# Layer 0 attention with two heads' scores in the two row halves of the array, and the side work at fixed places

## The chip, the cores and the metric

The kernel is one program on one core of a Trainium2 chip. It runs a diffusion backbone of two layers over 2048 latent tokens and 256 context tokens. The metric is the device time of one execution in microseconds (us). The engines have short names here: PE is the TensorE (its matmuls), PEld its weight loads, DVE the VectorE, ACT the ScalarE, POOL the GpSimd, and SP the engine that issues most DMAs. Matmul results are written to PSUM, which the kernel divides into 8 banks of 128 partitions by 512 fp32 values.

## The reference, cut to what matters

Layer 0 runs two mixers side by side on the same normalised input and adds their outputs through one output projection. Mixer A is attention with 8 heads; a query or key has 96 numbers, 64 without and 32 with a rotary part. Mixer B is linear attention in both directions with decay gates, in chunks.

```python
def mla_heads(q_lat, kv_lat, k_rope, q_norm, w_uq, kv_norm, w_ukv, q_gain, k_gain, rope):
    q = jnp.dot(rms_norm(q_lat, q_norm), w_uq).reshape(bsz, n, A_HEADS, A_QK)        # 8 heads x 96
    kv = jnp.dot(rms_norm(kv_lat, kv_norm), w_ukv).reshape(bsz, n, A_HEADS, A_NOPE + A_V)
    ...
    q = jnp.concatenate([q[..., :A_NOPE], apply_axial_rope(q[..., A_NOPE:], cos, sin)], axis=-1)
def block_attention(q, k, v, scale):
        s = jnp.einsum('bqhd,bkhd->bhqk', qi, k, preferred_element_type=jnp.float32) * scale
        p = jax.nn.softmax(s, axis=-1).astype(v.dtype)
        return jnp.einsum('bhqk,bkhd->bqhd', p, v)
def even_mixer(...):
    a_x = block_attention(q_x, [k_x, k_c], [v_x, v_c], scale)      # latent queries, all keys
    b_x, b_c = gla_bidirectional(gla_inputs(...), gla_inputs(...)) # mixer B
    y = jnp.dot(jnp.concatenate([a * silu(za), rms_norm(b) * silu(zb)], axis=-1), w_out)
    a_c = block_attention(q_c, k_c, v_c, scale)                    # context queries, context keys
# mixer B, one chunk: cumulative decay b, then
        att = jnp.where(mask, jnp.einsum('bhld,bhmd->bhlm', q_t, k_t), 0.0)
        o = jnp.einsum('bhld,bhde->bhle', q_t, state) + jnp.einsum('bhlm,bhme->bhle', att, vi)
        state = state * jnp.exp(b_last)[..., 0, :, None] + jnp.einsum('bhld,bhle->bhde', k_dec, vi)
```

## The kernel before, in words

**Precision.** A matrix product is made of reduced-precision fp32 parts: an operand is split into a high part and a low part, and a product is the sum of three matmuls, high by high, high by low and low by high.

**Stages.** `even_latent` makes queries and keys and writes them to the scratch tensors `QT` and `KT` in DRAM. `even_rest` makes the other projections and, woven into them, the row maxima of the scores (`maxes`); the negated maxima become row 96 of `QT`, and row 96 of `KT` holds ones, so that the first score matmul subtracts the maximum by itself. `even_mix` holds the stage that the change rewrites: attention (mixer A), mixer B (`gla`) and the splitting of the 16 units of `w_out` into high and low parts. Then `project` multiplies by `w_out`, and layer 1 follows.

**Attention, `even_attention`.** Heads go in 4 pairs `j`. Each pair has 5 query blocks `nb`: one of 256 context queries with 2 key tiles, and four of 512 queries with 18 key tiles of 128 keys each. That is 4 x (2 + 4 x 18) = 296 steps, and in each step both heads of the pair do one key tile. For one head a step has three matmuls into one PSUM bank `st` (L972 with 97 rows, L973 and L974 with 96 rows), one exponential on ACT into a tile `apt`, and on DVE one addition into the running sum `acc` (L963). `st` has 3 banks. When six steps are pending, four of them are multiplied with the values (L914, two heads in the two column halves of the array, plain fp32) into a bank `av`. `finish` (L842 to L857) takes the denominators with a matmul of the sums (L846, bank `den`), then Ln and Exp on ACT, three operations on DVE, one on POOL, and the store into `RT`. Two further banks, `gl`, belong to mixer B. Together these are 3 + 2 + 1 + 2 = 8 banks.

**Mixer B, `gla`.** 18 chunks of 128 tokens. `front` and `back` make a chunk's low-rank input (L714), gate logits (L720), log gates, cumulative decays (L731, L735), transposes (L758), masked scores within the chunk (L768, row halves of 64, plain fp32), values (L777) and state (L783). Then two scans run over the chunks, forward on POOL and backward on DVE (L806 to L808), and a second pass adds the carried state (L822), normalises, gates, and writes `RT`.

**Order.** `even_attention` is a generator: the code starts it, then emits all of `gla`, then the 16 weight splits, and then runs the rest of attention. A scheduler decides, from its own costs, where each instruction of these streams stands on its engine's queue. Every engine works its queue in order. `issue_after(x)` puts an instruction behind `x` on its engine. SP's queue is in order too, and in the built program each DMA on it waits until the eighth before it has landed.

Of the kernel before, what the change touches and what calls it, by code (L numbers as in the profile page):

```python
# [10 lines left out]
F32 = mybir.dt.float32  # L11
# [6 lines left out]
P = 128  # L18
# [70 lines left out]
class Kern:  # L89
# [311 lines left out]
    def even_latent(self, ws, wrest, kept):  # L401
        nc, tc = self.nc, self.tc
        self.QT = self.scr("QT", (A_HEADS, 2, A_QK + 1, T), F32)
        self.KT = self.scr("KT", (A_HEADS, 2, A_QK + 1, T), F32)
        self.Vn = self.scr("Vn", (P, NT, 512), F32)
        self.Un = self.scr("Un", (NT, P, 1568), F32)
        with ExitStack() as es:
# [34 lines left out]
            one = self.tl(sp, [P, Q_LORA], "sql", bufs=1)  # L442
            nc.gpsimd.memset(one[:8], 1.0)
            for o in range(0, T, Q_LORA):
                nc.sync.dma_start(self.KT[:, 0, A_QK, o : o + Q_LORA], one[:8])
# [104 lines left out]
            def fin(t):  # L550
                qn, kn = nat.pop(t)
                for z, (src, dst) in enumerate(((qn, self.QT), (kn, self.KT))):
                    col = 2 * z + (0 if t < NCT else 1)
                    for h2 in range(2):
                        ps = self.tl(pp, [P, 4, P], "tp")
                        for j in range(4):
# [6 lines left out]
                        nc.sync.dma_start(  # L563
                            dst[h2 * 4 : h2 * 4 + 4, :, :A_QK, t * P : t * P + P].rearrange("h s d t -> d (h s) t"),
                            hl[:A_QK].rearrange("d h s t -> d (h s) t").bitcast(F32))
# [42 lines left out]
    def even_rest(self, ws, win, hT):  # L608
        nc = self.nc
        self.zaT = self.scr("zaT", (4, P, T), F32)  # L610
        with ExitStack() as es:
# [33 lines left out]
            def maxes():  # L645
                for h in range(A_HEADS):
                    k = self.tl(sp, [P, T], "mk", F32R, bufs=2)
                    nc.sync.dma_start(k[:A_QK].bitcast(F32), self.KT[h, 0, :A_QK])
                    m = self.tl(sp, [P, NT, 5], "mm")
                    nc.vector.memset(m[:], -3e38)  # L650
                    for t in range(NT):
                        if t % 6 == 0:
                            q = self.tl(sp, [P, 768], "mq", F32R)
                            nc.sync.dma_start(q[:A_QK].bitcast(F32), self.QT[h, 0, :A_QK, t * P : t * P + 768])
# [13 lines left out]
                    nc.gpsimd.dma_start(self.QT[h, 0, A_QK].rearrange("(t p) -> t p", p=P), r[:NT].bitcast(F32))  # L668
# [9 lines left out]
    def gla(self, gp, gs, g1, gd, pp, tag):  # L678
# [25 lines left out]
        z4 = lambda a: a.rearrange("p (h z d) -> p h z d", z=2, h=H)  # L704

        def front(c):

            u = self.tl(g1, [P, 1056], "gu")
            nc.sync.dma_start(u[:], self.Un[c, :, :1056])
            gq, gk, gv = u[:, :256], u[:, 256:512], u[:, 512:1024]  # L710
            ps = bank()
            u3 = self.tl(gs, [P, 3, 32], "gu3")
            g.tensor_copy(u3[:], u[:, 1024:1056].unsqueeze(1).to_broadcast([P, 3, 32]))
            nc.tensor.transpose(ps[:96, :P], u3[:].rearrange("p n d -> p (n d)"), self.ident[:])  # L714
            r = rT[c % 2]
            self.act(r[:96, :], ps[:96, :P])
            nc.vector.tensor_tensor(out=r[32:64, :], in0=ps[32:64, :P], in1=r[32:64, :], op=ALU.subtract)
            yield
            lg = bank()
            nc.tensor.matmul(lg[:], r[:], gw[:], start=True, stop=True)  # L720
            e = self.tl(gs, [P, 512], "ge")
            self.act(e[:], lg[:], AF.Abs)
            self.act(e[:], e[:], AF.Exp, scale=-1.0)
# [65 lines left out]
        for _ in front(0):  # L789
            pass  # L790
# [946 lines left out]
```

## Time and profile before

The runs took 3657.13 us (median of 3, 3656.99 to 3663.05). The profiled execution spans 3650.5 us from its first to its last instruction.

| what | us |
|---|---|
| median of the runs | 3657.13 |
| span of the profiled execution | 3650.5 |
| latent stage (0 to 660 us) | 660 |
| rest and row maxima (660 to 1093.6) | 433.6 |
| attention with mixer B and the weight splits (1093.6 to 1974.1) | 880.5 |
| projection and layer 1 (1974.1 to the end) | 1676.4 |
| PE busy over the span | 3552.0 (97%) |

A row of a timeline gives the start and the length of an instruction, or of several that were merged (x8). Matmuls are pipelined, and the length of one reaches past the start of the next; what a matmul costs is therefore the distance between starts. "97*128" means 97 rows and 128 columns of the array, "97x512" the tile that moves through. In a row of a group stand its busy time, the mean of one in ns, the idle time of the engine just before it, and what ended that. A matmul in plain fp32 appears as two records.

### The profile page before, as it was taken

Reading aid. Unit: us, or ns where it says so; the run is one execution under the profiler, and the core shown is the slowest. Engines: PE = TensorE matmul, PEld = TensorE weight load, DVE = VectorE, ACT = ScalarE, POOL = GpSimd, SP = SyncE. Lnnn points to the kernel's source line nnn. Section 1 sums busy time; section 2 is a strip of 40 time slices with the busy share of each in tenths; the row PEclk is TensorE's granted clock in tenths of the full one; section 3 lists DMA queues with packets and bytes.
Section 4 is the critical chain, followed back from the end, with each engine's and each line's share of the span. In section 5 each row is a group of like instructions: output and inputs, shape, how many; then the busy total and the mean of one; then the engine's idle time right before and its main releaser. Section 6 shows DMA issues by size and latency. Waiting matters only on the chain. (4 is left out here: it accounts for less than half of the span.)

```text
span 3650.5 us, 51811 instructions
## 1 busy us (share of the span) xinstructions
PE 3552.0 (97%) x18404; PEld 2747.6 (75%) x18404; DVE 2355.2 (65%) x4846; ACT 1433.2 (39%) x2740; POOL 1234.9 (34%) x1376
## 2 busy tenths in 40 slices
PE   8999999999999999999999999999899999999899
PEld 6988987888886666665656887888788887555577
DVE  4677666888876766678765435455488784666732
ACT  5445551111115555555654214444422222555510
POOL 1433330101011211221311224333344442888763
PEclk9999999999999999999999999999999999999999
DMA  7455463222243232342632544545734446898672
GB/s 259 142 156 155 135 177 110 87 75 84 69 116 86 66 107 66 89 125 66 179 110 93 184 139 141 159 146 155 245 126 144 131 133 181 212 223 220 190 235 97
DMA packets 365780, 512.25 MB, mean 140 GB/s; under 512 B 26081, under 2 KB 245297, under 8 KB 359618
## 3 DMA queue, kind: packets, MB, share of 16 engines
q1 hardware_dynamic: 320754, 417.69, 39.3%
q0 software_dynamic: 22112, 63.26, 5.7%
q10 hardware_dynamic: 22656, 27.99, 2.2%
q8 instruction: 146, 2.39, 0.3%
q14 instruction: 112, 0.92, 0.1%
HBM read 329.45 MB, written 179.37 MB: 139 GB/s over the span
## 5 line engine op out<-in xcount | busy, mean ns | idle before, releaser
L963 DVE TENSOR_TENSOR acc<-acc,apt 128x512 f32<-128x512 f32 x512 | 375.6, 756 | 168.5 <-ACT apt L106 165.6
L106 ACT ACTIVATE apt<-st 128x512 f32<-128x512 f32 (+1 forms) x592 | 343.6, 594 | 290.7 <-PE st L974 262.0
L660 DVE TENSOR_REDUCE mm<-mx 128x1 f32<-128x512 f32 (+1 forms) x656 | 388.7, 629 | 87.3 <-PE mx L659 80.0
L914 PE MATMUL av<-apt,av 128*64 128x512 f32 (+1 forms) x1184 | 280.6, 594 | 0.0
L972 PE MATMUL st<-aq,akh 97*128 97x512 f32 (+1 forms) x592 | 256.6, 434 | 8.8 <-DMA aq<-QT 4.4
L659 PE MATMUL mx<-mk,mq 96*128 96x512 f32 (+1 forms) x656 | 235.8, 373 | 5.0 <-DMA mq<-QT 3.4
L1430 POOL TENSOR_TENSOR oacc<-oacc,opt 128x576 f32<-128x576 f32 (+5 forms) x192 | 223.0, 1184 | 39.7 <-ACT rl L106 19.3
L973 PE MATMUL st<-aq,akh 96*128 96x512 f32 (+1 forms) x592 | 235.5, 398 | 0.0
L1548 DVE TENSOR_TENSOR opt<-st,tab 128x64 f32<-128x64 f32 (+10 forms) x576 | 144.6, 317 | 140.3 <-PE st L1391 63.8
L974 PE MATMUL st<-aq,akl 96*128 96x512 f32 (+1 forms) x592 | 234.4, 396 | 0.0
L106 ACT ACTIVATE u<-gm 128x352 f32<-128x352 f32 (+1 forms) x140 | 68.6, 498 | 373.2 <-PE gm L131 210.6
L1307 DVE CUSTOM_DVE_ANT_1 mx<-mx,mtab 128x217 f32<-128x217 f32 (+12 forms) x576 | 184.2, 338 | 40.1 <-PE mx L1301 30.9
L914 PEld LDWEIGHTS av<-apt,av 128*64 128x64 f32 x1184 | 80.5, 137 | 153.6 <-issue 152.3
L972 PEld LDWEIGHTS st<-aq,akh 97*128 97x128 f32 x592 | 113.0, 191 | 99.1 <-issue 50.5
L106 ACT ACTIVATE opt<-opt 128x930 f32<-128x930 f32 (+7 forms) x129 | 104.2, 810 | 110.7 <-DVE opt L1548 102.6
L659 PEld LDWEIGHTS mx<-mk,mq 96*128 96x128 f32 x656 | 121.2, 188 | 16.8 <-DMA mk<-KT 3.8
L974 PEld LDWEIGHTS st<-aq,akl 96*128 96x128 f32 x592 | 113.9, 193 | 25.6
L973 PEld LDWEIGHTS st<-aq,akh 96*128 96x128 f32 x592 | 114.4, 193 | 17.1
L129 PE MATMUL gm<-w1h,hhi 128*128 128x512 f32 x288 | 116.3, 404 | 6.8 <-ACT onat L106 6.8
L106 ACT ACTIVATE x<-px,modB,modA 128x128 f32<-128x128 f32 x272 | 99.3, 468 | 56.9 <-PE px L339 54.4
L129 PE MATMUL gm<-w0h,hhi 128*128 128x512 f32 x288 | 116.3, 404 | 2.0 <-DVE hhi L351 1.9
L807 POOL TENSOR_TENSOR gsf<-gsf,D 64x512 f32<-64x512 f32 x17 | 25.1, 1477 | 271.4 <-DVE D L784 271.4
(492 smaller groups left out, 9962.1 us busy)
## 6 DMA issues: line engine op xcount, KB each, us to landing
q<-Q SPq DMA_DIRECT2D x48, 512.0 KB
H<-x ACTq DMA_DIRECT2D x36, 512.0 KB
adaw<-ada_w SPq DMA_DIRECT2D x64, 256.0 KB
x<-H SPq DMA_DIRECT2D x32, 512.0 KB
wraw<-w_od SPq DMA_DIRECT2D x64, 256.0 KB
K1t<-okt POOLq DMA_DIRECT2D x32, 512.0 KB, 7.6
kt<-K1t SPq DMA_DIRECT2D x32, 512.0 KB
mtab<-rpb_q SPq DMA_DIRECT2D x16, 899.0 KB
```

Source lines behind the costliest of these rows:

```text
L106: return self.nc.scalar.activation(out, in_, func, **kw)
L129: self.nc.tensor.matmul(out, lh(k), rh(k), start=j == 0, stop=False)
L659: mm = nc.tensor.matmul(ps[:, :w], q[:A_QK, (t % 6) * P : (t % 6) * P + P], k[:A_QK, k0 : k0 + w], start=True, stop=True)
L660: nc.vector.tensor_reduce(out=m[:, t, n : n + 1], in_=ps[:, :w], axis=AX.X, op=ALU.max)
L914: nc.tensor.matmul(O[j, nb][i * 64 : i * 64 + 64, :w], V[j, kt // TT][:, kt % TT, i * 64 : i * 64 + 64], pts[i][:, :w], start=n == 0, stop ...
L963: nc.vector.tensor_tensor(out=acc[i][:, :w], in0=a[:, :w], in1=pts[i][:, :w], op=ALU.add)
L972: nc.tensor.matmul(ps[:, :w], kh[: A_QK + 1, i, kq], qh[: A_QK + 1, :w], start=True, stop=False)
L973: nc.tensor.matmul(ps[:, :w], kh[:A_QK, i, kq], ql[:A_QK, :w], start=False, stop=False)
L974: mm = nc.tensor.matmul(ps[:, :w], kl[:A_QK, i, kq], qh[:A_QK, :w], start=False, stop=True)
L1307: nc.vector.tensor_tensor_reduce(out=s, in0=s, in1=tb[:, ri : ri + rn, ci : ci + cn], scale=1.0, scalar=-3e38, op0=ALU.add, op1=ALU.max, a ...
L1430: self.psum = nc.gpsimd.tensor_tensor(out=a, in0=a, in1=pts[:, :, a0 - r0 : a1 - r0, :], op=ALU.add)
L1548: bias = nc.vector.tensor_tensor(out=pt[:, d[0], d[1]], in0=ps[:, d[0], d[1]], in1=tabs[j][i][:, ri : ri + rn, ci : ci + cn], op=ALU.add)
```

## The change

**Scores.** Queries and keys are written to other scratch tensors: `QA`/`KA` (64 numbers without the rotary part), `QC`/`KC` (the 32 rotary numbers) and `QM` (the negated maxima). A pair's key tiles now hold head 0 in rows 0 to 63 and head 1 in rows 64 to 127. A step's score for one head is five matmuls with 64 rows (the last with 33): high by high, high by low and low by high of the 64 numbers; then the high rotary key, loaded twice, against the high and the low rotary query; then the low rotary key with the row of ones against the high rotary query with the row of maxima. The two heads' matmuls alternate between the two row halves and write two banks of one `st` tile. There are two such tiles (four banks). One ACT instruction makes both heads' exponentials (1024 columns), and one DVE instruction adds both heads' sums. For the context block nothing is added on DVE: its denominators are summed by PE.

**Places.** `gla` and the weight splits become a generator `side` that names the kind of place which its next piece wants. The cycle is four steps long: two steps, the place "middle", two steps, and `flush`, which has a place before the value matmuls ("before", "turn", "unit", "second") and one behind them ("after"). At a place the next piece is emitted if it wants that kind. A due denominator (`end`) stands in a flush too, and then a "second" piece waits. The denominators and the context block's output share the two banks `gl` with mixer B. Of a chunk, the place "before" takes `decays`, "turn" the transposes, "middle" the scores within the chunk, "after" the values, the forward scan, the low-rank input and the logits. The second pass takes one "second" place for each chunk. Each of the first 15 weight units takes one "unit" place; the sixteenth is split by `project`'s caller. What is left when attention ends is emitted behind it.

**Moved between engines.** Of mixer B, the copies of the low-rank input and of the values' output and the first step of the log gates go from ACT to DVE; the subtraction of the log gates, the addition of the two masked scores and the last operation of the backward scan go from DVE to POOL; the sum of squares goes from DVE to ACT (four instructions with an accumulator).

In the diff below, the first part makes the scratch tensors; the second, in `fin`, makes three stores of one; then come mixer B's pieces, the loads of a pair's keys (five for one; the low parts take three for one and the queries seven for two), `place` and `flush`, one step, and the weight units in `even_mix`. What was one load in the row maxima is two there.

```diff
-        self.QT = self.scr("QT", (A_HEADS, 2, A_QK + 1, T), F32)
-        self.KT = self.scr("KT", (A_HEADS, 2, A_QK + 1, T), F32)
+        self.QA, self.KA = [self.scr(n, (2, A_HEADS, A_NOPE, T), F32) for n in ("QA", "KA")]
+        self.QC, self.KC = [self.scr(n, (A_HEADS, 2, A_ROPE, T), F32) for n in ("QC", "KC")]
+        self.QM = self.scr("QM", (A_HEADS, T), F32)
...
-                        nc.sync.dma_start(
-                            dst[h2 * 4 : h2 * 4 + 4, :, :A_QK, t * P : t * P + P].rearrange("h s d t -> d (h s) t"),
-                            hl[:A_QK].rearrange("d h s t -> d (h s) t").bitcast(F32))
+                        for part in range(2):
+                            nc.sync.dma_start(da[part, hs, :, ts].rearrange("h d t -> d h t"), hl[:A_NOPE, :, part, :].bitcast(F32))
+                        nc.sync.dma_start(dc[hs, :, :, ts].rearrange("h s d t -> d (h s) t"),
+                                          hl[A_NOPE:A_QK].rearrange("d h s t -> d (h s) t").bitcast(F32))
...
+        for c in range(NT + 1):
+            if c:
+                yield "middle"
+                within(c - 1)
+            if c < NT:
+                yield "before"
+                decays(c)
+                softplus(c + 1)
+            if c:
+                yield "after"
+                values(c - 1)
+                scan(c - 1, slice(0, 64), g, g, "gsf")
+                inputs(c + 1)
+            if c < NT:
+                yield "turn"
+                turn(c)
+                yield "after"
+                low_rank(c + 3)
+                logits(c + 2)
+                fetch(c + 4)
...
+        for n in range(NT + 1):
+            yield "second"
+            if n:
+                write(order[n - 1])
+            if n < NT:
+                carried(order[n])
+                if n + 1 < NT:
+                    reads(order[n + 1])
+                squares(order[n])
+                if n + 1 < NT:
+                    back(order[n + 1])
+                gated(order[n])
...
+                dma(kh[:, 0, a:b], self.KA[0, 2 * j : 2 * j + 2, :, ts].rearrange("h d t -> (h d) t"))
+                for i in range(2):
+                    for o in (i * 64, i * 64 + 32):
+                        dma(kh[o : o + 32, 1, a:b], self.KC[2 * j + i, 0, :, ts])
...
+        def place(kinds, mm, *marks):
+            nonlocal want
+            if want not in kinds:
+                return mm
+            self.woven = mm
+            with ExitStack() as es:
+                for x in (mm, *marks):
+                    es.enter_context(self.tc.issue_after(x.ins))
+                want = next(side, None)
+            return self.woven
+
+        def flush(mm, *marks):
+            was, due = want, [x for x in late if x[0] or want != "before"]
...
+            mm = place(("before", "turn", "unit") if due else ("before", "turn", "unit", "second"), mm, *marks)
...
+                        mm = end(*x[1:])
...
+                        mm = tail(*p)
...
+            return place(("after",), mm, *marks)
...
-                    for i in range(2):
-                        qh, ql = Q[:, 2 * i, :], Q[:, 2 * i + 1, :]
-                        ps = self.tl(pp, [P, 512], "st", bufs=3)
-                        nc.tensor.matmul(ps[:, :w], kh[: A_QK + 1, i, kq], qh[: A_QK + 1, :w], start=True, stop=False)
-                        nc.tensor.matmul(ps[:, :w], kh[:A_QK, i, kq], ql[:A_QK, :w], start=False, stop=False)
-                        mm = nc.tensor.matmul(ps[:, :w], kl[:A_QK, i, kq], qh[:A_QK, :w], start=False, stop=True)
-                        pt = self.tl(ap, [P, 512], "apt", bufs=14)
-                        self.act(pt[:, :w], ps[:, :w], AF.Exp, scale=A_SCALE)
-                        pts.append(pt)
-                    add(n, pts)
+                    ps = self.tl(pp, [P, 2, 512], "st", bufs=2)
+                    terms = ((kh, 0, 0, 64), (kh, 0, 1, 64), (kl, 0, 0, 64), (kh, 1, 2, 64), (kl, 1, 3, 33))
+                    with self.tc.issue_after(mm.ins) if mm else ExitStack():
+                        for m, (k, kb, qb, r) in enumerate(terms):
+                            for o in (0, 64):
+                                mm = nc.tensor.matmul(ps[:, o // 64, :w], k[o : o + r, kb, kq], Q[o : o + r, qb, :w], start=m == 0, stop=m == 4)
+                    pts = self.tl(ap, [P, 2, 512], "apt", bufs=7)
+                    marks = [self.act(pts[:, :, :w], ps[:, :, :w], AF.Exp, scale=A_SCALE)]
...
+                    if len(pend) == 4:
+                        mm = place(("middle",), mm, *marks)
+                    elif len(pend) == 6:
+                        mm = flush(mm, *marks)
...
+                    for u in range(2 * KD):
+                        if waiting:
+                            self.split_unit(w, *waiting.pop())
+                        if u < 2 * KD - 1:
...
+                            waiting.append((u, self.load_unit(u, self.tl(g1, [P, 512], "gG", bufs=2)), place))
+                            yield "unit"
...
+            u = 2 * KD - 1
+            self.split_unit(w, u, self.load_unit(u, self.tl(sp, [P, 512], "py")), [self.tl(g1, [P, 512], "gG", F32R, bufs=2)[:] for _ in range(2)])
```

More of the change, by code (lines that the diff above doesn't have):

```diff
@@ L727, in front @@
             G4 = G[:].rearrange("p (h z d) -> p h z d", z=2, h=H)
-            yield
             mid = bank()
@@ L989, in even_attention @@
[L989 to L994 removed]
+                    if len(pend) == 4:
+                        mm = place(("middle",), mm, *marks)
+                    elif len(pend) == 6:
+                        mm = flush(mm, *marks)
+                    if nb == 4 and j < 3:
+                        if n == 2:
+                            for b in range(2):
+                                early[b], _ = queries(j + 1, b)
+                        if n % TT == TT - 1 and n < NT - 1:
+                            load(keys(j + 1, n // TT + 1), low(j + 1, n // TT))
@@ L996, in ln_exp @@
+        while pend or late:
+            mm = flush(mm, *marks)
+        for _ in side:
+            pass
     def ln_exp(self, after, es):
```

365 lines of the change are left out of this document (218 added, 147 removed).

## The prediction

> **What bounds the kernel now.** I read the page's totals first, then busy time by stage, then PE's timeline, the other engines' groups in the stage, and the places where PE is idle.
>
> ```profile
> span 3650.5 us, 51811 instructions
> PE 3552.0 (97%) x18404; PEld 2747.6 (75%) x18404; DVE 2355.2 (65%) x4846; ACT 1433.2 (39%) x2740; POOL 1234.9 (34%) x1376
> ...
> 1093.60:1974.10 880.50, 868.49 (x4229) 537.94 (x4227) 607.59 (x879) 479.92 (x956) 170.23 (x168) 0.99 0.33 93
> ```
>
> The third line is the attention stage: length, then busy time of PE, PEld, DVE, ACT and POOL, the clock, and the DMA share. PE is idle for 12.0 of 880.5 us at clock 0.99, so PE's own work is the bound there. DVE is busy 607.6 and ACT 479.9. Distances between starts on PE give what that work costs:
>
> ```profile
> 1499.26 1.16 PE L768 MATMUL gl<-gqT,gkT 64*128 64x128 f32 x16
> 1500.35 0.50 PE L972 MATMUL st<-aq,akh 97*128 97x512 f32 x1
> 1500.69 0.40 PE L973 MATMUL st<-aq,akh 96*128 96x512 f32 x1
> 1500.93 0.40 PE L974 MATMUL st<-aq,akl 96*128 96x512 f32 x1
> 1501.16 0.39 PE L972 MATMUL st<-aq,akh 97*128 97x512 f32 x1
> ...
> 1501.95 3.65 PE L914 MATMUL av<-apt,av 128*64 128x512 f32 x16
> 1505.53 0.50 PE L972 MATMUL st<-aq,akh 97*128 97x512 f32 x1
> ...
> 1507.27 1.05 PE L777 MATMUL gl<-gu,gat 128*128 128x128 f32 x8
> 1508.08 0.48 PE L972 MATMUL st<-aq,akh 97*128 97x512 f32 x1
> ```
>
> A score matmul of 512 columns costs 0.2335 us (1500.69 to 1501.16, two). Sixteen value records cost 3.58: in column halves, two records of 512 pass in 3.58/8 = 0.447, so each in 0.224. The row to watch is L768: sixteen records of 64 rows, in row halves, take 1.09 with the change of array mode on both sides, while L777's eight full-array records of the same width take 0.81. Sixteen in turn would take 1.6. So two row halves work at once, and a change of mode costs about (1.09 - 0.81 + 0.10)/2 = 0.19: 0.09 on entry, 0.34 for 0.235 on the next matmul.
>
> **Scores, the gain.** A head's step falls from three matmuls to five of half height, a pair's step from six passes to five double ones. Before: 288 steps x 6 = 1728 at 0.2335, and 48 of 256 columns at half that, 0.121 with its overhead: 409 us. After: 1440 pairs at 0.235 and 40 at 0.125: 343. That is -66. The pair's price is the term on which all hangs. Between column halves (0.224, half of the value rows' 0.447) and one after another (0.467) I take 0.235, since L768 is the nearest row: the same two halves, one extra pass hidden wholly.
>
> The Trainium skill, page "TensorE: Matmul & The Clock Gate", section "Part 3: Packing small matmuls — row/col tiling", speaks against a full gain: it reports four row tiles at 512 columns that come to about 3.07 times one, not four. By that rule a pair would be estimated at 0.2335 x 4/3.07 = 0.304, and the scores would cost 99 us more than in my sum. L768 shows no such loss, but at 128 columns only.
>
> **Switches and denominators.** In the order of instructions on PE the changes of mode fall from 259 to 239 in the stage: -20 x 0.19 = -4. The context blocks' denominators, summed by PE over two tiles for each head, add four groups of 0.5: +2. Together -68.
>
> **The exponential as a new wait.** These rows give ACT's delay and rate; the last two are 1024 wide, from the stage's end:
>
> ```profile
> 1501.36 1.29 ACT L106 ACTIVATE apt<-st 128x512 f32<-128x512 f32 x2 [1.40 <-PE st L974]
> ...
> 1095.74 0.38 ACT L106 ACTIVATE apt<-st 128x256 f32<-128x256 f32 x1
> ...
> 1096.17 0.38 PE L972 MATMUL st<-aq,akh 97*128 97x256 f32 x1 [1.36 <-ACT apt L106]
> ...
> L106 ACT ACTIVATE prh<-pr 128x1024 fp32r<-128x1024 f32 x1 | 1.1, 1062 | 3.7 <-DMA pr<-RT 3.7
> ...
> L1075 DVE TENSOR_TENSOR px<-pr,prh 128x1024 fp32r<-128x1024 f32 x1 | 1.2, 1226 | 4.0 <-ACT prh L106 4.0
> ```
>
> ACT starts 0.43 after the start of the last matmul (1500.93), and PE restarts 0.05 after an exponential ends (1096.12 to 1096.17). With two `st` tiles, step n+2 waits for the exponential of step n: from that step's start 0.94 to its last pair, 0.43, 1.02, 0.05 make 2.44, against 2 x 1.175 = 2.35. Where nothing stands between four steps, that is 0.1, and as much again for a first matmul that starts cold: 0.2 x some 56 cycles without "middle" = +11. With three banks of 512 before, this slack was far larger. Below: 0, if ACT's lead is 0.1 shorter.
>
> **DVE, POOL and mixer B.** ACT and DVE lose no work by the wider forms, but DVE's queue is now written out by hand, and in the second pass of mixer B a chain runs through it once in a cycle:
>
> ```profile
> L823 DVE TENSOR_TENSOR goi<-gl,goi 128x512 f32<-128x512 f32 x18 | 12.4, 688 | 0.5 <-PE gl L822 0.4
> L830 DVE TENSOR_TENSOR goi<-goi,gss 128x512 f32<-128x512 f32 x18 | 12.3, 683 | 0.9 <-POOL gss L210 0.9
> L806 DVE TENSOR_TENSOR gsb<-gsb,fac 64x512 f32<-64x512 f32 x17 | 11.7, 690 | 0.7 <-POOL fac L740 0.2
> L745 DVE TENSOR_TENSOR gqt<-gqt,gu 128x512 f32<-128x512 f32 x18 | 22.3, 1238 | 3.7 <-ACT gqt L106 3.7
> ...
> L208 POOL TENSOR_SCALAR gss<-gss 128x4 f32<-128x4 f32 x18 | 8.5, 475 | 107.9 <-DVE gss L827 107.9
> L210 POOL TENSOR_TENSOR gss<-gss,mhalf 128x4 f32<-128x4 f32 x18 | 22.4, 1242 | 1.5
> ...
> 1701.47 1.14 ACT L106 ACTIVATE gsb<-gl,gn 128x128 f32<-128x128 f32 x4
> ```
>
> Four sums at 1.23 to 1.33, one scan step 0.69, the addition of the carried state 0.69, then the multiplication by `gss` (0.68), which stands behind four small squares on ACT (1.14, if they cost what four scaled copies do) and behind POOL's two operations (0.48 and a power of 1.24). With half an exponential in ACT's way (0.5), DVE's cycle comes to 10.3 to 10.9. PE's cycle there is 4 x 1.175, 3.58, 0.81 and 0.45 for mixer B's matmuls and transposes and two changes: 9.95. I take +0.65 x 18 = +12. Queued behind the waiting multiplication are the next four sums, so `apt` tiles come free late, ACT waits for one, PE for ACT. In the first pass a chunk takes two cycles; counted in the same way, DVE's two (eight sums, two rotations by L745's kind, the mask products, the copies) end within 0.3 of PE's, with the subtraction and the mask addition moved to POOL: 18 x 0.3 = +5. Each denominator, and each context output, now takes a `gl` bank that ACT or DVE must first empty; a copy-out of 0.69 for the 13 of 24 that fall where mixer B also asks for one: +9; none, if they fall between its pieces.
>
> **The start.** The order on SP puts the load of `gw`, which needs an ACT copy, ahead of the second half of the low rotary keys, which the first step's last matmul needs; seven query loads of the first 512 block stand behind that.
>
> ```profile
> 1093.58 0.28 PE L972 MATMUL st<-aq,akh 97*128 97x256 f32 x1
> ...
> 1094.44 1.28 ACT L999 ACT_TABLE_LOAD   x1
> ...
> 1097.78 0.40 SPq L877 DMA_DIRECT2D akh<-KT  x1
> ...
> 1114.66 0.60 SPq L689 DMA_DIRECT2D gw<-gw  x1
> ...
> 1613.38 0.33 SPq L388 DMA_DIRECT2D wraw<-w_out  x1
> ...
> 1616.05 0.63 ACT L106 ACTIVATE gG<-wraw 128x512 fp32r<-128x512 f32 x1 [1.40 <-DMA wraw<-w_out]
> ```
>
> Before, `gw` was loaded 20 us into the stage. After, ACT's copy ends after the table load, at about 1096.2; six issues at 0.4 follow, and a landing of 2.67 (1613.38 to 1616.05): the low keys at about 1101. PE has 1 us of scores by then: 7 idle, 1.9 more for the queries, against 1.36 of before, and colder matmuls for 2: +9. If the copy stood early: +1.
>
> **The end.** Only five of the sixteen weight units are split before the last exponentials. A unit's round is 2.67 for the load, 0.63 on ACT, 0.69 on DVE: 4.0, with two buffers 2.0 a unit, so the last of 11 is ready 22 later, its three matmuls 0.7 after. PE has 4.6 of values and denominators and 11.2 of the first tile: 22.7 - 15.8 = 7, and cold matmuls 2: +9. If the cover is better: 0.
>
> **What goes.** The idle 12.0 of before were scattered, one of them so:
>
> ```profile
> 1624.54 0.80 PE L972 MATMUL st<-aq,akh 97*128 97x512 f32 x1 [2.34 <-ACT apt L106]
> 1625.13 0.63 PE L973 MATMUL st<-aq,akh 96*128 96x512 f32 x1
> 1625.56 0.63 PE L974 MATMUL st<-aq,akl 96*128 96x512 f32 x1
> ```
>
> ACT was held by a weight load, and the matmuls behind it start 0.59 and 0.43 apart instead of 0.235. The fixed places end these: -12 and some 6 of such cold matmuls, -18. The 144 more stores in the latent stage cost 144 x 0.33 = 48 of SP's time. I put that at 0: SP spends more than this there waiting for DVE:
>
> ```profile
> SPq L563 <- DVE qkhl L561: 104.3, 44, 15.6
> ```
>
> The other DMAs (queries seven for two, keys five for one, low keys three for one, two for one in the row maxima) are issued ahead of need, and cost nothing but at the start; without that cover the 32 more of the maxima alone would be 32 x 0.33 = 11. The scan operation and the copies of `rT` and `goi` that change engine are in the cycles above.
>
> **The sum.** -68 + 11 + 12 + 5 + 9 + 9 + 9 - 18 = -31. The span falls from 3650.5 to 3619.5. The runs' median lies 6.6 above the span of the profiled execution, so 3626.
>
> **Rivals.** A, the sum above. B, the places hide nearly all the new waits: only start and end (+18) stay of the 54, and the idle of before goes: -68 + 18 - 18 = -68, 3589. For it speaks that ACT and DVE have 400 and 270 us free in the stage; against it the 0.1 by which the exponential is late. C, the row halves slow each other at 512 columns, since both stream 512 columns of fp32 through the array and write two banks: it decides from a pair at 0.235 + 31/1440 = 0.257. Halfway to one after another, 0.35, it gives 3626 + 166 = 3792; wholly in series 3960. L768 speaks against it, without settling the width. By the Trainium skill's section on packing, named above, the time would be an estimated 3725. D, on the other side with one mechanism: the sums of 1024 on DVE slow down beside POOL, as L745 does (1238 where its like take 690), and POOL has more to do now. At 1.5 instead of 1.23 the four sums add 1.1 to DVE's cycle, which then passes PE's in the 55 cycles that hold a piece of mixer B; it decides from 31/55 = 0.56 a cycle, and gives 3626 + 60 = 3686. Against it stands L963 of before:
>
> ```profile
> L963 DVE TENSOR_TENSOR acc<-acc,apt 128x512 f32<-128x512 f32 x512 | 375.6, 756 | 168.5 <-ACT apt L106 165.6
> ```
>
> Its mean is only 756, beside a POOL that was a fifth busy (170.2 of 880.5).
>
> **How the numbers follow.** A 0.57, B 0.19, C 0.08, D 0.16. The likeliest alone lies within 3600 to 3648. The range runs to 3570 (B, and pairs at 0.224: 3573) and to 3688 (D). C is left out. About 0.2% (7 us) is what a measurement of this kernel tells from no change. Faster: A but for its upper edge, and B, 0.72; same 0.06; slower: C, D, 0.22.
>
> **What would show it.** Right: starts of a pair of L1121 0.235 apart; the stage some 850 us long; idle time ahead of L1121 named ACT, 0.1 at a time; first 512-column scores near 1103; eleven splits after the last exponential. D shows as `acc` sums of 1.5 us and more and ACT waiting for DVE; C as pairs above 0.257. Wrong in any case, if the latent stage grows past 660.

## The result and the profile after

The changed kernel takes 3632.81 us (median; 3631.16 to 3635.78), the kernel before 3657.06 in the runs beside it (3656.09 to 3663.05). The ratio is 0.9929, with a 95% interval of 0.9915 to 0.9943. The profiled execution spans 3632.5 us; an execution takes 1.8 us more than its span (3634.33 for 3632.5), so the profile of before (3650.5) is that of an execution some 5 us faster than the median, and the two profiles differ by 18.0 where the medians differ by 24.3.

From the page, and from the table by stage (length, then busy time of PE, PEld, DVE, ACT and POOL, the clock, the DMA share), here attention and all that follows it:

```profile
span 3632.5 us, 53914 instructions
PE 3489.4 (96%) x19604; PEld 2693.3 (74%) x19604; DVE 2346.1 (65%) x4567; ACT 1391.7 (38%) x2516; POOL 1344.5 (37%) x1430
```

```profile
1099.10:1945.50 846.40, 796.39 (x5429) 480.43 (x5428) 591.45 (x591) 432.45 (x723) 281.19 (x221) 0.99 0.35 106
1945.50:3632.50 1687.00, 1639.56 (x8402) 1273.32 (x8400) 963.98 (x2591) 604.90 (x1022) 823.26 (x772) 0.99 0.59 172
```

PE's busy time in attention fell by 72.1 (868.5 to 796.4), but its idle time there grew from 12.0 to 50.0, so the stage is only 34.1 shorter. What follows attention is 10.6 longer (1676.4 to 1687.0), and attention begins 5.5 later (1093.6 to 1099.1). That is -34.1 + 10.6 + 5.5 = -18.0.

The 50.0 us have names. Of what PE waited for in attention (us in total, times, the longest), this is the whole list:

```profile
PE st L1121 <- DMA akl<-KC: 16.1, 1, 16.1
PE gl L823 <- DVE goi L819: 13.3, 17, 0.8
PE gl L883 <- POOL goi L876: 10.7, 12, 1.2
PE gl L948 <- ACT gqT L106: 4.7, 8, 0.6
PE st L1121 <- ACT apt L106: 2.5, 2, 2.0
PE st L1121 <- DVE u L626: 1.5, 1, 1.5
PE gl L762 <- DVE ge L805: 1.1, 1, 1.1
```

The price of a pair, from PE's timeline over two steps in a row (x4 are two pairs, x2 is one), the first pair of the next step with its weight load, and ACT's exponentials beside them:

```profile
1227.62 0.63 PE L1121 MATMUL st<-aq,akh 64*128 64x512 f32 x4
1228.09 0.39 PE L1121 MATMUL st<-aq,akl 64*128 64x512 f32 x2
1228.32 0.39 PE L1121 MATMUL st<-aq,akh 64*128 64x512 f32 x2
1228.55 0.39 PE L1121 MATMUL st<-aq,akl 33*128 33x512 f32 x2
1228.91 0.30 PEld L1121 LDWEIGHTS st<-aq,akh 64*128 64x128 f32 x4 [0.40 <-ACT apt L106]
1228.91 0.73 PE L1121 MATMUL st<-aq,akh 64*128 64x512 f32 x4
1229.47 0.39 PE L1121 MATMUL st<-aq,akl 64*128 64x512 f32 x2
...
1227.83 2.19 ACT L106 ACTIVATE apt<-st 128x1024 f32<-128x1024 f32 x2 [0.76 <-PE st L1121]
```

Pairs start 0.23 apart (1227.62, two pairs, 1228.09; then 1228.32, 1228.55): two row halves at 512 columns cost one pass. In the records the two matmuls of a pair mostly start 0.003 to 0.004 apart. The third step of a run comes 0.36 after the last pair of the second and not 0.23, and its own first pair costs 0.33: the exponential of the first step, which began at 1227.83 and takes 1.08, has just ended. PE's list of waits does not show this, because a matmul's length reaches past the start of the next. It shows in the starts, and in the weight load of that step, which names the exponential. Of 202 places in the records where a step follows a step directly, 56 are above 0.25; they cost 7.4 us, and the cold pairs behind them 5.8.

### The profile page after: what moved, and what is told of

Its sections match the earlier page's. It is cut to its first block, busy times and chain, and to the rows that moved or that the text cites. A ratio compares the mean times of both kernels' runs of the same rounds, so it can differ in the third digit from the quotient of the medians.

```text
span 3632.5 us, 53914 instructions
## 1 busy us (share of the span) xinstructions
PE 3489.4 (96%) x19604; PEld 2693.3 (74%) x19604; DVE 2346.1 (65%) x4567; ACT 1391.7 (38%) x2516; POOL 1344.5 (37%) x1430
## 5 line engine op out<-in xcount | busy, mean ns | idle before, releaser
L1128 DVE TENSOR_TENSOR acc<-acc,apt 128x1024 f32<-128x1024 f32 x256 | 362.9, 1417 | 85.2 <-ACT apt L106 66.7
L106 ACT ACTIVATE apt<-st 128x1024 f32<-128x1024 f32 (+1 forms) x296 | 300.3, 1015 | 237.2 <-PE st L1121 217.2
L1121 PE MATMUL st<-aq,akh 64*128 64x512 f32 x1728 | 312.2, 410 | 2.7 <-ACT apt L106 2.5
L1032 PE MATMUL av<-apt,av 128*64 128x512 f32 x1152 | 263.2, 598 | 0.0
L1121 PE MATMUL st<-aq,akl 64*128 64x512 f32 (+1 forms) x1152 | 230.0, 392 | 0.0
L1121 PEld LDWEIGHTS st<-aq,akh 64*128 64x128 f32 x1728 | 151.0, 186 | 86.6 <-ACT apt L106 30.1
L1121 PEld LDWEIGHTS st<-aq,akl 64*128 64x128 f32 (+1 forms) x1152 | 110.4, 185 | 24.4 <-DMA akl<-KC 0.3
L210 POOL TENSOR_TENSOR oss<-oss,mhalf 128x8 f32<-128x8 f32 x68 | 113.2, 1665 | 5.1
L130 PE MATMUL gm<-w1l,hhi 128*128 128x512 f32 x288 | 114.9, 399 | 0.0
L131 PE MATMUL gm<-w1h,hlo 128*128 128x512 f32 x288 | 114.2, 397 | 0.0
```

The source lines that it names most:

```text
L106: return self.nc.scalar.activation(out, in_, func, **kw)
L130: self.nc.tensor.matmul(out, lh(k), rl(k), start=False, stop=False)
L131: yield self.nc.tensor.matmul(out, ll(k), rh(k), start=False, stop=j == n - 1)
L1032: mm = nc.tensor.matmul(O[j, nb][i * 64 : i * 64 + 64, :w], V[j, kt // TT][:, kt % TT, i * 64 : i * 64 + 64], pts[:, i, :w], start=n == 0, ...
L1121: mm = nc.tensor.matmul(ps[:, o // 64, :w], k[o : o + r, kb, kq], Q[o : o + r, qb, :w], start=m == 0, stop=m == 4)
L1128: added = nc.vector.tensor_tensor(out=acc[:, :, :w], in0=a[:, :, :w], in1=pts[:, :, :w], op=ALU.add)
```

## Experiments

Since executions differ by some 3 us in the stages before attention, each effect is read below in the stage it belongs to, and the medians stand beside it. A stage is read from one profile of each kernel. In the four profiles of kernels with the old attention, that stage took 878.1 to 881.0, so an effect of 3 in it is hardly told from none, unless its place in the stage can be named. The part behind attention took 1681.4 to 1691.1 in the six profiles that share it.

**Set-up behind the first loads.**

```diff
-        want = next(side)
+        want = None
...
                 for g in gens:
                     next(g)
+                want = next(side)
                 for p in (1, 2):
```

> The changed kernel with one line moved: mixer B's set-up (its loads of the gate weights, masks and first inputs) is emitted behind the second halves of the first keys and the first 512 queries, so that SP no longer holds those behind the load that waits for ACT's gw. Theory (order on SP): the 16.1 us for which PE waited for akl<-KC fall under 3, the granted clock stays near 1.0 at the start of the stage, and the time falls by 15 to 19, to about 3616. Rival (the small transfers of 32 rows and POOL's memsets of akl are slow in themselves): the wait stays above 10, and the time falls by less than 5.

The median was 3620.19, 12.6 below the changed kernel (ratio to before 0.990, interval 0.9885 to 0.9915). The wait for `akl<-KC` is gone whole, and attention is 12.2 shorter (834.2). Five of the gain came back, in ACT's queue:

```profile
1108.01 0.63 ACT L106 ACTIVATE gw<-ge 97x512 fp32r<-97x512 f32 x1 [4.91 <-DMA ge<-gate_w]
1108.54 1.92 ACT L106 ACTIVATE apt<-st 128x1024 f32<-128x1024 f32 x2
```

The `gw` copy waits 4.91 for its load, and two exponentials stand behind it. So the order on SP was what held PE, as the theory had it, but the slow load of the gate weights is a second cause beside it.

**The gate weights as 96 rows and one.** In the changed kernel the load `ge` was issued at 1099.08, and this is what followed (SP's issue, ACT's copy, SP's next issue; then the table of four-us windows as above):

```profile
1099.08 0.24 SPq L687 DMA_DIRECT2D ge<-gate_w  x1
...
1110.07 0.63 ACT L106 ACTIVATE gw<-ge 97x512 fp32r<-97x512 f32 x1 [8.81 <-issue]
...
1110.73 0.58 SPq L690 DMA_DIRECT2D gw<-gw  x1
```

```profile
1106.00:1110.00 4.00, 0.00 (x0) 0.00 (x0) 0.00 (x0) 0.00 (x0) 0.00 (x0) 0.50 0.06 25
...
1118.00:1122.00 4.00, 4.00 (x25) 3.35 (x25) 0.00 (x0) 1.45 (x3) 0.00 (x0) 0.53 0.83 246
```

From 1106 to 1110 no engine works, and the DMA engines are 0.06 busy, one of sixteen, at 25 GB/s. At that rate the 194 KB of `ge` take some 8 us. PE's clock is at 0.50 there, and still at 0.53 when matmuls run again.

```diff
-        nc.sync.dma_start(raw[:97], self.i["gate_w"])
+        for a, b in ((0, 96), (96, 97)):
+            nc.sync.dma_start(raw[a:b], self.i["gate_w"][a:b])
```

> The changed kernel with the load of the gate weights (97 rows of 2 KB) made in two pieces, 96 rows and one. In the changed kernel ACT's gw copy comes 11.0 after the load's issue, and from 1106 to 1110 the DMA engines are 0.06 busy at 25 GB/s, which is one of sixteen. Theory (the 97-row load runs through one DMA engine, and that is what makes the start 16 and not the predicted 7): ge lands within 3.5 of its issue, gw's load is issued by about 5 after ge's, PE's wait for akl<-KC falls from 16 to 6 to 9, and the time falls by 7 to 10, to about 3624. Rival (the small transfers of tri, ind and gn around it fill the queues): ACT's copy still comes 9 or more after the issue, and the time changes by less than 2.

The median was 3625.31, 7.5 lower (ratio to before 0.9918, 0.9901 to 0.9935); attention fell by 8.5 to 837.9, and PE's wait from 16.1 to 7.9:

```profile
1098.56 0.65 SPq L688 DMA_DIRECT2D ge<-gate_w  x2
...
1100.86 0.63 ACT L106 ACTIVATE gw<-ge 97x512 fp32r<-97x512 f32 x1
...
1101.51 0.57 SPq L691 DMA_DIRECT2D gw<-gw  x1
```

The copy now comes 2.3 after the issue, right behind the table load, as the prediction had placed it, and the wait of 7.9 is the predicted 7. The Trainium skill, page "DMA: Bandwidth & Descriptors", section "Why a DMA increments its semaphore by 16 and not by 1", says that a transfer is spread over the largest number of engines up to 16 that divides the slowest dimension on both its sides; by that rule 97 rows go through one engine and 96 through sixteen. The 25 GB/s, the 0.06 and the 2.3 agree with it.

**Two buffers for `gkt`.** The rows of a chunk in the changed kernel:

```profile
1219.45 0.59 ACT L106 ACTIVATE gqt<-gl 128x512 f32<-128x512 f32 x1
...
1223.33 1.16 PE L817 MATMUL gl<-gu,gat 128*128 128x128 f32 x8
1224.52 0.69 DVE L819 COPY goi<-gl 128x512 f32<-128x512 f32 x1 [1.20 <-PE gl L817]
...
1225.27 1.16 PE L823 MATMUL gl<-gu,gkt 128*128 128x128 f32 x8 [0.78 <-DVE goi L819]
...
1226.46 0.60 ACT L106 ACTIVATE gkt<-gl 128x512 f32<-128x512 f32 x1 [5.61 <-PE gl L823]
```

ACT empties the bank of the decays in two steps, `gqt` at 1219.45 and `gkt` only at 1226.46, since the one `gkt` tile is still read by L823. Until then values (L817) and state (L823) share the other bank, with DVE's copy between them.

```diff
-            kt = self.tl(g1, [P, 512], "gkt", bufs=1)
+            kt = self.tl(g1, [P, 512], "gkt", bufs=2)
...
-                    places = [(g1, t) for t in ("gqt", "gkt", "gkT", "gat", "tri")] + ...
+                    places = [(g1, t) for t in ("gqt", "gkt", "gkt", "gkT", "gat", "tri")] + ...
```

> The changed kernel with two buffers for gkt (and one for the last unit's wo tiles, to make room). Theory: in the changed kernel ACT cannot write the next chunk's gkt before the state matmuls L823 have read the old one, so the bank of the decays is not emptied, and values and state must share the other bank, with DVE's copy between them; with two buffers the 17 waits of 0.78 of L823 go and the time falls by 12 to 14, to about 3620. Rival (DVE's copy itself, moved there from ACT, is what comes late, whichever bank): the 17 waits stay at 0.4 to 0.8 and the time falls by less than 5.

The median was 3613.19, 19.6 lower (ratio to before 0.9879, 0.9865 to 0.9894). The 17 waits are gone from the list, and attention is 18.9 shorter (827.5). Set against each other chunk by chunk, the two kernels drift apart by 1.05 at each L823: the idle 0.78, and 0.28 for matmuls that no longer start cold. Over the 17 chunks that is 17.9, more than the 12 to 14 expected. The rival is out.

**Transposes of the second pass behind the values.** One cycle of the changed kernel in the second pass, in order of time:

```profile
1642.92 6.01 DVE L1128 TENSOR_TENSOR acc<-acc,apt 128x1024 f32<-128x1024 f32 x4 [1.62 <-ACT apt L106]
...
1645.45 1.16 PE L857 MATMUL gl<-D,gqT 128*128 128x128 f32 x8
1646.54 3.65 PE L1032 MATMUL av<-apt,av 128*64 128x512 f32 x16
1648.85 0.68 DVE L858 TENSOR_TENSOR goi<-gl,goi 128x512 f32<-128x512 f32 x1
...
1651.27 1.05 POOL L839 TENSOR_TENSOR D<-gsb,fac 64x512 f32<-64x512 f32 x1
...
1652.40 1.05 POOL L210 TENSOR_TENSOR gss<-gss,mhalf 128x4 f32<-128x4 f32 x1
...
1653.48 0.69 DVE L875 TENSOR_TENSOR goi<-goi,gss 128x512 f32<-128x512 f32 x1 [2.51 <-POOL gss L210]
...
1654.25 2.18 POOL L876 TENSOR_TENSOR goi<-goi,gsf 128x512 f32<-128x512 f32 x1 [0.81 <-DVE goi L875]
...
1656.48 0.66 PE L883 MATMUL gl<-ident,goi 128*128 128x128 f32 x4 [1.17 <-POOL goi L876]
```

L857 has done by 1646.5, but L858 stands behind four sums, until 1648.85; on POOL the scan step that was moved there (L839, 1.05) stands ahead of the power (L210); and the last product runs beside DVE's sums and takes 2.18, where its mean before was 1.31. At the end PE waits for it.

```diff
             yield "second"
-            if n:
-                write(order[n - 1])
             if n < NT:
                 carried(order[n])
...
                 gated(order[n])
+                yield "after"
+            if n:
+                write(order[n - 1])
```

> The changed kernel with the output transposes of mixer B's second pass (L883) emitted behind the value matmuls and not ahead of them. Theory: PE waits 12 times, 10.7 us in all, for POOL's gated product, because the chain through DVE, ACT, POOL, DVE, POOL is about a microsecond longer than the cycle; 3.6 us later in the cycle nothing waits, and the time falls by 9 to 11, to about 3623. Rival (DVE's queue is the bound of that pass): the wait moves to the exponentials, through late sums and full apt buffers, and the time falls by less than 4.

PE's 12 waits for POOL are gone, yet attention is only 3.2 shorter (843.2). PE's waits for the exponential rose from 2.5 to 5.7, and the transposes at the new place need one more change of array mode in each of 18 cycles, an estimated 3.4 at 0.19: -10.7 + 3.2 + 3.4 = -4.1. Set against each other step by step, the kernel gains 4.8 within the second pass; 1.6 it had lost before it, at a place where the kernel of `ge96`, which has no edit there, loses 1.7. The median, 3624.75, is 8.1 lower (ratio to before 0.9915, 0.9898 to 0.9931); its profile owes 3.5 of its smaller span to an earlier begin and 5.6 to what follows attention, which the edit does not touch. Each theory is half right: the chain was the cause of the wait, and 3.2 of it moved to the exponentials; the other 3.4 are the price of this edit and not a limit of the kernel.

**Weight units at three places of the cycle.**

```diff
-                        mm = place(("middle",), mm, *marks)
+                        mm = place(("middle", "unit"), mm, *marks)
...
-            return place(("after",), mm, *marks)
+            return place(("after", "unit"), mm, *marks)
```

> The changed kernel with the weight units taken at three places of a cycle (before the values, after them, and in the middle) where it was one. Theory (the 11 units that are split after the last exponential are what stretches the projection's beginning): the idle time ahead of the first projection matmuls falls from 9 to under 1, and the time by 9 to 11, to about 3623. Rival (the splits take as much from attention's last cycles as they free, on ACT through the loads' latency): ACT's exponentials are late there, and the time changes by less than 3.

The median was 3627.18, 5.6 lower (ratio to before 0.992, 0.9906 to 0.9935). What follows attention fell by 6.4 (1687.0 to 1680.6; its first part, the projection, by 10.3), but attention grew by 3.2 (849.6). PE's timeline of the changed kernel at the projection's begin, then ACT's of this kernel in attention's last cycles:

```profile
1952.94 0.50 PE L130 MATMUL pj<-D,prh 128*128 128x512 f32 x1 [0.44 <-DVE D L1235]
...
1956.79 0.49 PE L129 MATMUL pj<-D,prh 128*128 128x512 f32 x1 [1.97 <-ACT D L106]
```

```profile
1932.66 0.63 ACT L106 ACTIVATE D<-gG 128x512 fp32r<-128x512 f32 x1 [3.27 <-DMA gG<-w_out]
1933.20 1.92 ACT L106 ACTIVATE apt<-st 128x1024 f32<-128x1024 f32 x2
```

A split that waits for its load holds the exponentials behind it. Of attention's 3.2, though, 1.3 arose in its first 30 us, before any unit is split, and 1.9 in the last cycles, so about a fifth of the projection's gain was paid back. Theory and rival both count; the 5.6 lies between their numbers.

**One head's five matmuls ahead of the other's.**

```diff
-                        for m, (k, kb, qb, r) in enumerate(terms):
-                            for o in (0, 64):
+                        for o in (0, 64):
+                            for m, (k, kb, qb, r) in enumerate(terms):
```

> The changed kernel with the five score matmuls of one head ahead of the five of the other, where the two heads alternated; the same matmuls in the same two row halves. Theory (two row halves work at once only when their matmuls stand next to each other in PE's order): each matmul costs 0.23 to 0.24 on its own, a step 2.3 instead of 1.17, and the time rises by 288 x 1.15 = 330, to about 3960. Rival (PE looks ahead in its queue and runs the other half's matmuls early): the starts of one head's matmuls fall between the other's, and the time changes by less than 20.

One execution took 3672.97, and attention 883.5, 37 more, not 330. PE's timeline of a step and the begin of the next:

```profile
1231.96 0.84 PE L1121 MATMUL st<-aq,akh 64*128 64x512 f32 x3
1232.53 0.39 PE L1121 MATMUL st<-aq,akl 64*128 64x512 f32 x1
1232.64 0.52 PE L1121 MATMUL st<-aq,akh 64*128 64x512 f32 x2
1232.87 0.52 PE L1121 MATMUL st<-aq,akl 64*128 64x512 f32 x2
1233.11 0.51 PE L1121 MATMUL st<-aq,akh 64*128 64x512 f32 x2
1233.34 0.40 PE L1121 MATMUL st<-aq,akl 33*128 33x512 f32 x1
```

In the order of the program each head goes `akh`, `akh`, `akl`, `akh`, `akl`, and in the built program all 296 steps have five matmuls of one half ahead of five of the other. Three `akh` ran before the first `akl`, and afterwards two matmuls start every 0.23: the second head started beside the first one's second matmul, though it stands behind its fifth. The first theory falls. The rival's mechanism holds, though not its "less than 20". With the second head a matmul or so behind, a step's exponential starts that much later; that this makes up the 37 was not tried.

**The stages before attention.** Two edits of the kernel before: `stores` has the three stores of `fin`, `stores2` also the loads of the row maxima in two pieces; `plain` is the kernel before.

```diff
-                        nc.sync.dma_start(dst[h2 * 4 : h2 * 4 + 4, :, :A_QK, ...].rearrange("h s d t -> d (h s) t"), ...)
+                        for part in range(2):
+                            nc.sync.dma_start(dst[hs, part, :A_NOPE, ts].rearrange("h d t -> d h t"), hl[:A_NOPE, :, part, :].bitcast(F32))
+                        nc.sync.dma_start(dst[hs, :, A_NOPE:A_QK, ts].rearrange("h s d t -> d (h s) t"), ...)
```

> The kernel before, with each store of queries and keys in fin made in three pieces (high part of the 64 numbers, low part, rotary numbers), into the same tensors: 144 more issues on SP in the latent stage, as the change has them, and nothing else. Theory (SP waits for DVE there anyway, so the issues are free): the stages before attention end within 1 of those of the kernel before, and the time is within 3 of it. Rival (the three stores are what makes the changed kernel reach attention 2 to 5.5 later): attention begins at 1096 to 1099 instead of 1093.6, and the time rises by 3 to 5.

> The kernel before, unchanged, for a second profile of it. If the two stages before attention vary by themselves, attention begins some us away from 1093.6, in the range 1095.6 to 1099.1 of the five profiles of changed kernels; if the later begin belongs to the change, it begins at 1093 to 1094.5.

> The kernel before with the three stores of fin and also with the loads of the row maxima in two pieces, 64 rows and 32, as the change has them; same tensors. Theory (the doubled loads of the maxima are what delays the begin of the row maxima by 3 to 4): the first row-maximum matmul starts near 565 and attention near 1097. Rival (it is in something else that the change brought into the stages before attention, or in nothing but where they happen to fall): near 561 and 1094, as in the three profiles of kernels of the old layout.

Attention began at 1092.7 with `stores` (ratio to before 0.9994, 0.9985 to 1.0004), at 1095.4 with `plain`, at 1095.6 with `stores2` (its row maxima at 563.6). The 144 more issues cost nothing. The four profiles of the old layout begin between 1092.7 and 1095.6, mean 1094.3; the ten of the new one between 1095.1 and 1099.1, mean 1097.1. So the change costs about 3 there, not 5.5; the loads of the maxima may be a part of it, but one profile between the two forecasts does not settle it.

**All edits together.** `best` has the five edits above, and takes a due denominator behind the second value tile; `best2` leaves the transposes where they were; `best3` leaves the denominators too.

```diff
-                for x in due:
-                    with self.tc.issue_after(mm.ins):
-                        mm = end(*x[1:])
-                    late.remove(x)
                 short = None
                 for n in range(5):
+                    if n == 2 or not pend:
+                        for x in due:
+                            ...
+                        due = []
```

> The changed kernel with all the single edits together: mixer B's set-up behind the first loads, the gate weights loaded as 96 rows and one, two gkt buffers, the second pass's transposes behind the values, weight units at three places, and due denominators behind the second of the value tiles instead of ahead of the first. Theory (each wait has its own cause, so the gains add): attention falls by 17 (start) + 19 (gkt) + 3 (transposes) + 5 (denominators, 8 waits of 0.6) and the projection by 7 to 10, 52 in all: about 3581. Rival (the same slack is counted several times, and the exponentials or DVE become the bound): less than 35 of it is left, above 3598.

> As the kernel with all edits, without the one on the second pass's transposes. Theory (moving them costs a further change of array mode in each of 18 cycles, 3.4 in all, and the exponentials come late instead): 2 to 4 slower than with it, about 3584. Rival (with the other waits gone, the transposes behind the values only cost): equal or faster by up to 4.

> As the kernel with all edits, without the one on the transposes and without the one on the denominators: set-up behind the first loads, gate weights as 96 rows and one, two gkt buffers, weight units at three places. Theory (the later denominators are what ate the rest: their three operations on DVE then stand ahead of the low-rank copies of the next logits, and cost 0.9 to 1.5 each, against 0.6 to 0.9 gained): attention 812 to 816 and the span near 3587, 5 or more below the other two. Rival (the single gains share slack, whatever the set): attention 819 to 822 again, span 3591 to 3594.

Medians 3596.93, 3599.5 and 3596.68; ratios to before 0.9836 (0.982 to 0.9852), 0.9842 (0.9827 to 0.9856) and 0.9845 (0.9828 to 0.9861). Against the changed kernel that is 33 to 36 less, about a third short of the 52 forecast from the single gains; on `best` the rival (above 3598) missed by 1 and the theory (3581) by 16. Attention took 819.2, 820.9 and 818.1. That `best2` is 2.6 slower than `best`, as its theory had it, is not told from no difference: the intervals overlap nearly whole. The longest of PE's waits in `best3`:

```profile
PE gl L884 <- POOL goi L877: 10.5, 12, 1.2
PE st L1123 <- ACT apt L106: 4.9, 3, 2.7
PE gl L949 <- ACT gqT L106: 4.7, 8, 0.6
```

So the edits on transposes and denominators take waits away without making the kernel faster: 10.5 and 4.7 of waits stand here, and the time is the same. `best3` shows where the rest of its own sum went. Set against the two-buffer kernel, it gains 17 at the start and keeps it until the second pass ends, then loses 7.4 where the weight units hold ACT, and wins 6.9 back in the projection: the edit on the units is worth nothing here. Of the two theories on `best3` the rival was right in the span (3593.8) and nearer in attention (818.1, where it had 819 to 822 and the theory 812 to 816).

## Why the prediction was right, and where its terms were not

The forecast was 3626 and faster; 3632.81 lies in its range and in the likeliest case's own. That the mechanism was the one forecast shows in the pairs and in the named waits; that the total came so near is in part luck, as the last point of this list says. Point by point:

- **Scores, -66: right.** A pair cost 0.232, not more than one pass, at 512 columns too, and rival C is out. The Trainium skill's figure for four row tiles in "TensorE: Matmul & The Clock Gate", section "Part 3: Packing small matmuls — row/col tiling", from which 0.304 had been estimated, does not carry over to these two halves.
- **The exponential as a new wait, +11: right**, 56 places and 13.2 us, though it hides in PE's busy time.
- **The second pass of mixer B, +12: right in size (10.7), wrong in its last link.** The step said that the sums come late, and through them `apt`, ACT and PE. It was PE's own transposes that waited for the product. The way that was forecast stood behind it: with the first wait gone, 3.2 came back as waits for the exponential. (Added up again, the step's cycles are 10.3 to 10.7 for DVE and 9.92 for PE, and make it +11.)
- **The first pass, +5: the step that failed most.** It counted DVE's work against PE's cycle; the loss was 13.3 of idle time, 17.9 with cold matmuls, and came from a single buffer. A count of an engine's work does not see two results that must share a bank.
- **Shared banks, +9: mis-sized;** 4.7 for denominators and 1.1 elsewhere.
- **The start, +9: mis-sized; it was 16.** The place was right, the landing of `ge` was not: 11.0 instead of the 2.67 of another load. With the load repaired, PE waited 7.9.
- **The end, +9: right;** 10.1 in the projection (198.3 to 208.4), with ten splits behind the last exponentials. In four other kernels with the same end the projection took 205.7 to 207.0, so 7 to 10.
- **What goes, -18:** of the idle time before, only the 2.5 for exponentials is left, -9.5; the cold matmuls were not counted apart.
- **The latent stage, +0:** right for the stores; some 3 came from elsewhere. By its letter a sign of being wrong came true, a stage that grows past 660: the transpose that ends the row maxima of the first head came 4.9 later, before and after:

```profile
646.02 0.28 PE L665 MATMUL mx<-ident,mc 128*18 128x128 f32 x1
650.90 0.28 PE L666 MATMUL mx<-ident,mc 128*18 128x128 f32 x1
```

But kernels of the old layout had it at 645.0 to 647.9 and those of the new one at 646.9 to 650.9, so the sign was too sharp for what it measured.

- **D: its premise came true, its forecast did not.**

```profile
L1128 DVE TENSOR_TENSOR acc<-acc,apt 128x1024 f32<-128x1024 f32 x256 | 362.9, 1417 | 85.2 <-ACT apt L106 66.7 <-DVE acc L1128 0.9
```

The sums slowed to a mean of 1.42, but DVE still idled 85 us ahead of them, mostly for ACT's exponentials, so DVE did not become the bound. In the second pass, however, a slowed sum and the slowed product stand in the chain that PE waits for; how much of the 10.7 is theirs was not tried. The mean of 756 ns, by which D was held to be unlikely, hid what was there before: 414 sums with no POOL work beside them took 0.69 on average, the 130 others 0.95.

- **What the sum left out.** Adding up PE's records in attention, each from its start to the next one's without the idle time, gives a fall of 72 where the sum's terms for that (-68, +11 and -6 for cold matmuls) make -63. The scores fell by 76, although the 13.2 are in them; the values fell by 13 and the masked scores within a chunk by 7, and mixer B's other pieces grew by 24, and these three were in no term. The idle time grew by 38, where the terms (+12, +5, +9, +9, -12) make 23. So the sum had 9 too little gain and 15 too little loss in this stage, and the two partly cancelled.

B, that the places would hide nearly all waits, was wrong for this kernel: with start, end and `gkt` mended, 3597 was reached, near B's 3589, which still has the losses at start and end in it.

The 6.6 between span and runs was wrong as well: 1.8 belong to every execution, the rest to a fast execution before.

## What to carry to other kernels

When work is moved from a scheduler's hands to fixed places, go through each place and ask which single buffer or bank two neighbours share, and what stands ahead of the consumer on the same queue; that found more here than adding up engine time. A wait of 0.1 between back-to-back matmuls is missing from PE's list of waits; look for it in the distances between starts and in the waits of the weight loads. And a wait that can be named is not yet a gain: 15 us of PE's waits could be removed without making the kernel faster.

## What the hardware showed that was not expected

- Matmuls in the two row halves ran as two streams: a half's first matmul started three matmuls ahead of its place, each half 0.23 from start to start.
- A load of 97 rows of 2 KB was used 11.0 us after its issue and moved at 25 GB/s; as 96 rows and one it was used 2.3 after.
- The clock granted to PE was 1.00 until some 3 us after the last matmul and 0.50 from then on; it stayed there for the first 4 us of matmuls after the wait (in windows of one us, 0.50 from 1105 to 1121 and 1.00 from 1122).
- DVE and POOL slowed each other. The 150 sums of 128x1024 with no POOL work beside them took 1.21 to 1.23 us, the 122 others 1.64 on average and up to 2.26; of the four that took 6.01, one took 2.02 and three 1.23. POOL's product took 2.18 there, against a mean of 1.31 before.
